# Moving A's norms and transposes, B's first operands and C's heads in the order in which a two-layer encoder trunk is emitted

## The chip, the cores and the metric

The kernel runs on one core of one Trainium2 chip. The metric is the device time of one execution in microseconds (us), as a median of several runs. TensorE (PE in the rows; PEld is its weight load) multiplies matrices into PSUM, VectorE (DVE) and ScalarE (ACT) read PSUM and work elementwise, GpSimd (POOL) works elementwise on SBUF alone, and SyncE's queue (SPq) starts the DMAs.

## The reference

A trunk of two layers over x of 512 rows and 1024 columns, in float32. Each layer normalises x, projects it once and feeds three attention branches with the parts of the projection. Their outputs are gated, merged and projected, a squared-ReLU MLP follows, and a final norm ends the trunk.

```python
for l in range(DEPTH):                      # DEPTH = 2
    h = _rms_norm(x, ln1_g[l])
    proj = jnp.einsum('bsd,dn->bsn', h, w_in[l])
    (a_q, a_k, a_v, b_q, b_k, b_v, c_cq, c_ckv, c_kr, gate_logits) = _split_columns(proj)
    y_a = _gqa_axial(...)        # 8 q heads, 2 kv heads, width 64: RMS norm of q and k per head, rotary, softmax
    y_b = _diff_attention(...)   # 8 heads, two softmaxes of width 32 each, p0 - lam * p1
    y_c = _mla(...)              # q and k, v from normalised ranks 384 and 256; a rotary part of 32 beside 64
    gates = jax.nn.sigmoid(gate_logits.reshape(b, s, N_BRANCH, d))
    merged = jnp.sum(gates * jnp.einsum('bsne,ned->bsnd', y, w_branch[l]), axis=2)
    x = x + jnp.einsum('bsd,de->bse', merged, w_out[l])
    h2 = _rms_norm(x, ln2_g[l])
    ff = jnp.square(jax.nn.relu(jnp.einsum('bsd,df->bsf', h2, w_ff1[l])))
    x = x + jnp.einsum('bsf,fd->bsd', ff, w_ff2[l])
return _rms_norm(x, final_g)
```

## The kernel before

**Numbers.** Every float32 operand of a matmul is split into a high part (a cast to the matmul's float32r, `hi`, on ScalarE) and a low part (operand less high part, `lo`, on VectorE). A product is three matmuls: high by high, high by low, low by high. A weight is fetched by SyncE into `wr` (2 buffers), cast by ScalarE into `wh` (L61) and subtracted into `wl` (L67), by VectorE in one piece of 1024 columns or by GpSimd in four of 256; `POOLW` of every five weights go to GpSimd.

**The plan.** `plan` (L996) makes a list of items, each with a cost in us of TensorE's time, a function that emits its instructions, and its weights. `run` (L153) goes through the list with a clock `t` that adds the costs. Ahead of each item it emits weight fetches up to 8 us and splits up to 3 us ahead, then all functions whose due time has come (`tick`), then the item. `defer(dt, f)` enters f with due time t + dt. `want(d, k)` (L146) runs the entered functions in the order of their due times until key k is there. `weave` mixes a list of attention items with a list of matmul items in proportion to their costs. All this sets the order of emission. The tile framework takes the emitted instructions, finds what depends on what, and lays down the order of each engine.

**Stages of a layer.** First A's k, v and C's rotary key in one projection (`a_kv`, L520, eight items of 1.458 us), then q of A's two groups (`a_q`, L482, two times eight items of 1.296), then q and k of B's first half (`b_qk`). A's scores (`att_a`, 32 items of 1.3) are woven with the rest of B's projections, B's scores (`att_b`) with the first gates and C's ranks, rotated q (`c_rope`), first values (`c_v`) and first pair, C's scores (`att_c`) with the other pairs of heads and gates. Output and MLP follow.

**A's q.** When a group's four PSUM tiles are read, `post` rotates it (`a_rope`, L453: multiplications by two tables on VectorE, half of them on GpSimd). `LAG_Q` = 14 us later `late` (L505) transposes it on TensorE (`transpose4`, L320, four matmuls each into a PSUM tile of tag T, of which there are two) and writes each pair of heads' `a_G`: two reads by ScalarE, two subtractions by VectorE (L216). At its end `late` calls `norm` (L497): the squares on GpSimd (L477), a sum on VectorE (L479), one operation (L500) and eleven small ones of `rsqrt` (L230 to L241). The result `aR[g]` is first used as the scale of the probabilities (L575, L576).

**A's k.** `post` of `a_kv` norms and rotates k and leaves `a_kr` (L549); `LAG_KV` = 14 us later `late` (L552) transposes it and splits it into `a_K` (L211 on ScalarE, L218 on VectorE).

**B.** `b_stack(h)` (L704) puts together the operands of head h, twelve DMAs from SBUF to SBUF for `b_sq` and `b_sk`. The first item of `att_b` emits `b_stack(0)` and `b_stack(1)`, the first item of each later head the next one.

**C.** `c_rope` projects the rotary part of q, rotates it (`c_t`, L880), and 6 us later transposes and splits it into two tiles `c_qr`. `c_pair(j)` (L901) projects two heads of q (`uq`) and of k (`uk`), each into a PSUM tile of tag L, of which there are three; the gates, branches and value chunks use the same three. For each head it reads the head's half of the tile two times on ScalarE, subtracts once on VectorE and copies the rotary part in by DMA.

Of the kernel before, what the change touches and what calls it, by code (L numbers as in the profile page):

```python
# [127 lines left out]
class Trunk:  # L128
# [353 lines left out]
    def a_q(self, l, g):  # L482

        nc = self.nc
        st = {}

        def evac(tt, ps):
            if tt == 0:
                st["t"] = self.s4("a_tq", (128, 4, 256), F32)
            nc.scalar.copy(st["t"][:, tt], ps)  # L490

        def post():
            t1, t2 = self.a_rope(st["t"], 4, "q")
            nc.vector.tensor_tensor(t1, t1, t2, op=ALU.add)
            st["r"], st["f"] = t1, t2

        def norm():  # L497
            ss = self.head_sumsq(nc.gpsimd, st["t"], st["f"], 4)
            v = ss.rearrange("p (t h) -> p t h", h=4)
            nc.vector.scalar_tensor_tensor(  # L500
                v, v, 1.0 / 64, self.evar.unsqueeze(2).to_broadcast([128, 4, 4]), op0=ALU.mult, op1=ALU.add)
            self.aR[g] = self.p.tile([128, 16], F32, tag="a_R", name="a_R", bufs=2)
            self.rsqrt(self.aR[g], ss, 16)

        def late():  # L505
            for j in range(2):
                T = self.transpose4(st["r"], slice(j * 128, (j + 1) * 128))
                G = self.s4("a_G")
                self.hi(G[0:64, 0], T[0:64])
                self.hi(G[64:128, 1], T[64:128])  # L510
                self.lo(G[64:128, 0], T[0:64], G[0:64, 0])
                self.lo(G[0:64, 1], T[64:128], G[64:128, 1])
                self.aG[2 * g + j] = G
            norm()

        k = P_TM[f"q{g}"]
        return self.tm_chunk([self.big(l, k), self.big(l, k + 1)], 4, 256, "x", evac, post, late, self.LAG_Q,
                             self.TAGQ if g == 0 else "LL")

# [115 lines left out]
    def att_a(self):  # L635
        self.y = {}

        def probs(h, qt):
            g, j, e = h // 4, h // 2, h % 2
            q = slice(qt * 128, (qt + 1) * 128)  # L640
            G, K = self.want(self.aG, j), self.want(self.aK, g)
            i = qt * 4 + h % 4
            p, z = self.probs([(G[:, e, q], K[:, 0]), (G[:, e, q], K[:, 1])], self.aR[g][:, i : i + 1])
            self.normalise(p, z)
            return p

        def vt(h):
            o = 64 * (h % 2)
            return lambda k: self.aV[h // 4][:, k, o : o + 128]

        return self.attend(probs, vt, self.finish_plain("a"), 1.3)
# [63 lines left out]
    def att_b(self, l):  # L715
        nc = self.nc

        def probs(h, qt):

            if h == 0 and qt == 0:  # L720
                self.b_stack(0)
            if qt == 0 and h < 7:
                self.b_stack(h + 1)
            q = slice(qt * 128, (qt + 1) * 128)
# [138 lines left out]
    def c_rope(self, l):  # L863
# [22 lines left out]
                self.split(f, T)  # L886
                self.qr[j] = f

        return self.tm_chunk([Weight(self, self.a["w768"][3 * l + 2], 768)], 3, 256, "q", evac, post, late, 6.0)

    def c_v(self, l, hb):
        def evac(tt, ps):
# [8 lines left out]
    def c_pair(self, l, j):  # L901
# [5 lines left out]
        def q():  # L907
            ps = self.ps("L", "uq")
            self.mm(ps, self.fm_pairs(w, 0, self.want(self.cf, "q")))
            for e in range(2):  # L910
                Q = self.s4("c_Q")
                r, o = (slice(0, 64), slice(64, 128)) if e == 0 else (slice(64, 128), slice(0, 64))
                self.hi(Q[r, 0], ps[r])
                self.hi(Q[r, 1], ps[r])
                self.lo(Q[o, 0], ps[r], Q[r, 0])
                h = 2 * j + e
                rr = (h % 4) * 32
                for part in range(2):
                    self.copy(Q[o.start + 32 * part : o.start + 32 * part + 32, 1], self.want(self.qr, h // 4)[rr : rr + 32, part])
                self.cQ[h] = Q  # L920

        def k():
            ps = self.ps("L", "uk")
            self.mm(ps, self.fm_pairs(wk, 0, self.want(self.cf, "kv")))
            for e in range(2):
                K = self.s4("c_K")
                r, o = (slice(0, 64), slice(64, 128)) if e == 0 else (slice(64, 128), slice(0, 64))
                self.hi(K[r, 0], ps[r])
                self.hi(K[o, 0], ps[r])
                self.lo(K[r, 1], ps[r], K[r, 0])  # L930
                self.copy(K[o, 1], self.kr[o, 0])
                self.cK[2 * j + e] = K

        return [(9 * 0.216, q, [w]), (6 * 0.216, k, [wk])]

    def att_c(self):
        def probs(h, qt):
            q = slice(qt * 128, (qt + 1) * 128)
            Q, K = self.cQ[h], self.cK[h]
            p, z = self.probs([(Q[:, 0, q], K[:, 0]), (Q[:, 1, q], K[:, 1]), (Q[:, 1, q], self.krl[:, h % 2])],  # L940
                              self.rq[:, qt : qt + 1])
            self.normalise(p, z)
# [53 lines left out]
    def plan(self, l):  # L996
# [29 lines left out]
        fb1 = self.b_qk(l, "q", 1) + self.b_qk(l, "k", 1) + self.b_v(l, 1)  # L1026
        r += fb[: self.FB]
        r += [(0, lambda: setattr(self, "POOLW", self.PA), [])]
        r += weave(self.att_a(), fb[self.FB :] + fb1)
        gb = [[self.gate_branch(l, n, d) for d in range(8)] for n in range(3)]  # L1030
        att = self.att_b(l)
        gates = lambda n, d0, d1: sum(gb[n][d0:d1], [])
# [176 lines left out]
    def go(self):  # L1209
# [5 lines left out]

        self.AHEAD_F, self.AHEAD_S = 8.0, 3.0
        self.LAG_T, self.LAG_V, self.LAG_C = 5.5, 6.0, 9.0
        self.LAG_Q, self.LAG_KV, self.LAG_R = 14.0, 14.0, 60.0

        self.P0, self.PA, self.PF = 1, 5, 0  # L1220
        self.FB = 16
# [134 lines left out]
```

## Time and profile before

| | us |
|---|---|
| median of 3 runs | 1881.75 (1879.80 to 1882.43) |
| profiled execution | 1881.45 |
| its span, first to last instruction | 1879.70 |
| TensorE busy | 1821.7 |
| VectorE busy | 1422.4 |
| ScalarE busy | 1009.8 |
| GpSimd busy | 398.3 |

The profile is one execution on the chip. A view of waits names an engine's instruction, what ended the idle time in front of it, the total, the number of times and the longest. A timeline gives start and duration of merged instructions in us, the line of the kernel, the operation, the tile written and the tiles read, the shape and the count; idle time in front stands in brackets with its releaser. A releaser is inferred from semaphores: where it names the reader of a PSUM tile, the instruction waited for that tile to come free.

### The profile page before, as it was taken

The page shows a single profiled execution, that of the slowest core. Times are in us where ns is not written, and L with a number is a line of the kernel's source. Part 1 is how long each engine was busy: PE and PEld are TensorE (multiplying, and loading weights), DVE is VectorE, ACT ScalarE, POOL GpSimd, SP SyncE. Part 2 cuts the span into 40 slices and gives each one's busy share as a digit, 9 for nine tenths or more (in the row PEclk, how much of TensorE's full clock was granted, in tenths as well). Part 3 has the DMA queues.
Part 4 walks back from the last instruction along what each step waited for, and adds up shares of the span by engine and source line. Part 5 has one row for each costly group of instructions (what it writes and reads, how often), then busy time and mean ns, then how long its engine had stood idle before and what let it go on. Part 6 is the DMA issues. An engine that isn't in the chain of part 4 may idle for free.

```text
span 1879.7 us, 29631 instructions
## 1 busy us (share of the span) xinstructions
PE 1821.7 (97%) x10960; PEld 1600.8 (85%) x10960; DVE 1422.4 (76%) x2815; ACT 1009.8 (54%) x1828; POOL 398.3 (21%) x493
## 2 busy tenths in 40 slices
PE   8999999999999999999999999999999999999997
PEld 8998787777888898989899988778878888989897
DVE  7888889755665776868888888896556767778687
ACT  5577666655544434444445766665554444443553
POOL 4322433444101000000043224434440000000000
PEclk9999999999999999999999999999999999999999
DMA  5213341332153232242332134312232522423321
GB/s 163 79 40 85 102 107 43 96 88 86 40 180 90 74 118 82 88 139 74 98 106 69 46 94 120 90 48 85 84 90 67 164 90 68 135 62 120 114 77 62
DMA packets 67776, 172.06 MB, mean 92 GB/s; under 512 B 10032, under 2 KB 14512, under 8 KB 67632
## 3 DMA queue, kind: packets, MB, share of 16 engines
q1 hardware_dynamic: 67632, 170.16, 30.3%
q8 instruction: 87, 1.43, 0.3%
q14 instruction: 57, 0.47, 0.1%
HBM read 149.15 MB, written 4.19 MB: 82 GB/s over the span
## 4 chain that ended last, share of the span: by engine, by line
PE 72%; DVE 15%; ACT 5%; DMA 4%; issue 3%; POOL 1%; SPq 0%; DVEq 0%; ACTq 0%; POOLq 0%
PE ff L208 19%; PE gate L208 12%; PE ff L1136 11%; PE br L208 6%; PE tm L295 4%; PE out L208 4%; PE sc L208 4%; PE pv L208 4%; PE pT L587 3%; DMA wr<-w 2%; PE c_rank L208 2%; DVE fl L99 2%; DVE fa L93 1%; DVE wl L67 1%; DVE mx L571 1%
## 5 line engine op out<-in xcount | busy, mean ns | idle before, releaser
L67 POOL TENSOR_TENSOR wl<-wr,wh 128x256 fp32r<-128x256 f32 (+1 forms) x402 | 297.7, 770 | 541.2 <-ACT wh L61 523.8
L61 ACT CAST wh<-wr 128x1024 fp32r<-128x1024 f32 (+5 forms) x246 | 224.6, 914 | 344.4 <-PE ff L208 94.0
L1136 PE MATMUL ff<-h,fh 128*128 128x256 f32 x1792 | 327.7, 285 | 3.7 <-ACT fh L98 3.5
L208 PE MATMUL ff<-xg,wh 128*128 128x512 f32 x1024 | 316.1, 390 | 1.8 <-ACT wh L61 1.8
L1136 PEld LDWEIGHTS ff<-h,fh 128*128 128x128 f32 x1792 | 281.0, 192 | 6.9 <-ACT fh L98 5.7
L1136 PE MATMUL ff<-h,fl 128*128 128x256 f32 x896 | 255.2, 286 | 3.0 <-DVE fl L99 3.0
L208 PE MATMUL gate<-xg,wh 128*128 128x512 f32 x768 | 242.6, 394 | 1.1 <-DVE c_K L216 1.1
L98 ACT CAST fh<-fa 128x640 fp32r<-128x640 f32 (+1 forms) x168 | 125.4, 762 | 206.8 <-PE ff L1136 122.1
L208 PEld LDWEIGHTS ff<-xg,wh 128*128 128x128 f32 x1024 | 191.6, 188 | 41.9 <-ACT wh L61 2.6
L338 POOL TENSOR_TENSOR acc<-acc,sq 128x512 f32<-128x512 f32 x15 | 25.4, 1695 | 834.8 <-ACT sq L336 832.3
L208 PE MATMUL ff<-xg,wl 128*128 128x512 f32 x512 | 199.7, 390 | 2.1 <-DVE wl L67 2.1
L295 PE MATMUL tm<-wh,xg 128*128 128x256 f32 x1024 | 201.6, 288 | 0.0
L571 DVE TENSOR_REDUCE mx<-sc 128x1 f32<-128x512 f32 x256 | 173.8, 683 | 36.3 <-PE sc L208 35.3
L1136 PEld LDWEIGHTS ff<-h,fl 128*128 128x128 f32 x896 | 172.1, 192 | 5.2 <-DVE fl L99 4.5
L208 PEld LDWEIGHTS gate<-xg,wh 128*128 128x128 f32 x768 | 143.6, 189 | 30.2 <-PE pv L208 1.4
L67 DVE TENSOR_TENSOR wl<-wr,wh 128x1024 fp32r<-128x1024 f32 (+3 forms) x117 | 134.1, 1146 | 42.6 <-ACT wh L61 42.3
L295 PEld LDWEIGHTS tm<-wh,xg 128*128 128x128 f32 x1024 | 163.9, 191 | 0.2
L99 DVE TENSOR_TENSOR fl<-fa,fh 128x640 fp32r<-128x640 f32 (+1 forms) x168 | 143.3, 864 | 10.3 <-ACT fh L98 10.3
L208 PE MATMUL gate<-xg,wl 128*128 128x512 f32 x384 | 150.9, 393 | 0.0
L590 ACT CAST pt<-pT 128x512 fp32r<-128x512 f32 x192 | 111.8, 585 | 64.3 <-PE pT L587 62.3
L591 DVE TENSOR_TENSOR pt<-pT,pt 128x512 fp32r<-128x512 f32 x192 | 131.3, 686 | 19.6 <-ACT pt L590 17.9
L295 PE MATMUL tm<-wl,xg 128*128 128x256 f32 x512 | 144.7, 283 | 0.0
(246 smaller groups left out, 3530.2 us busy)
## 6 DMA issues: line engine op xcount, KB each, us to landing
wr<-w SPq DMA_DIRECT2D x170, 512.0 KB, 3.6
fa<-wff SPq DMA_DIRECT2D x64, 320.0 KB, 3.1
wr<-w SPq DMA_DIRECT2D x52, 256.0 KB, 2.8
fa<-wff SPq DMA_DIRECT2D x32, 384.0 KB, 3.3
b_sq<-b_f SPq DMA_DIRECT2D x96, 64.0 KB, 3.0
b_sk<-b_f SPq DMA_DIRECT2D x96, 64.0 KB, 2.0
x<-xT SPq DMA_DIRECT2D x8, 256.0 KB, 5.5
c_Q<-c_qr SPq DMA_DIRECT2D x32, 64.0 KB, 2.9
```

The lines of the kernel that those rows point to most:

```text
L61: t.nc.scalar.copy(wh, self.raw)
L67: e.tensor_tensor(wl[:, q], self.raw[:, q], wh[:, q].bitcast(F32), op=ALU.subtract)
L98: t.nc.scalar.copy(h, x)
L99: t.nc.vector.tensor_tensor(lo, x, h.bitcast(F32), op=ALU.subtract)
L208: self.nc.tensor.matmul(out, l, r, start=(i == 0), stop=(i == n - 1))
L295: self.nc.tensor.matmul(ps, l, r, start=(u == 0 and i == 0 and tt % 2 == 0), stop=(u == 1 and tt % 2 == 1 and i == len(p) - 1))
L338: e.tensor_tensor(st[d % 2], st[d % 2], sq, op=ALU.add)
L571: nc.vector.tensor_reduce(m, s, axis=AX.X, op=ALU.max, negate=True)
L587: nc.tensor.transpose(T[:, k], p[:, k * 128 : (k + 1) * 128], self.ident)
L590: nc.scalar.copy(h[:, :, q], T)
L591: nc.vector.tensor_tensor(lo[:, :, q], T, h[:, :, q].bitcast(F32), op=ALU.subtract)
L1136: nc.tensor.matmul(bk[tag], x, y, start=(new and a == 0), stop=(part[1] == n and a == len(pairs) - 1), skip_group_check=True)
```

## The change

- `LAG_KV` goes from 14.0 to 16.5, the lag of `c_rope` from 6.0 to 8.0.
- `norm` of A's q is no longer called at the end of `late` but entered with a due time 6 us later. `att_a` asks for `aR` by `want`.
- `b_stack(0)` is emitted as an item of its own, three items ahead of the end of the woven list of A's scores, instead of in the first item of B's scores.
- In `c_pair` both rotary tiles of q are asked for ahead of the heads. The first head of q and of k is emitted at once, the second 2.5 us later. `att_c` asks for `cQ` and `cK` by `want`.

```diff
@@ a_q, late @@
                 self.aG[2 * g + j] = G
-            norm()
+            self.defer(6.0, norm)
@@ att_a, probs @@
-            p, z = self.probs([(G[:, e, q], K[:, 0]), (G[:, e, q], K[:, 1])], self.aR[g][:, i : i + 1])
+            R = self.want(self.aR, g)
+            p, z = self.probs([(G[:, e, q], K[:, 0]), (G[:, e, q], K[:, 1])], R[:, i : i + 1])
@@ att_b, probs @@
-            if h == 0 and qt == 0:
-                self.b_stack(0)
@@ c_rope @@
-        return self.tm_chunk([Weight(self, self.a["w768"][3 * l + 2], 768)], 3, 256, "q", evac, post, late, 6.0)
+        return self.tm_chunk([Weight(self, self.a["w768"][3 * l + 2], 768)], 3, 256, "q", evac, post, late, 8.0)
@@ c_pair, q @@
-            for e in range(2):
+            want = [self.want(self.qr, (2 * j + e) // 4) for e in range(2)]
+
+            def head(e):
                 Q = self.s4("c_Q")
...
-                    self.copy(Q[o.start + 32 * part : o.start + 32 * part + 32, 1], self.want(self.qr, h // 4)[rr : rr + 32, part])
+                    self.copy(Q[o.start + 32 * part : o.start + 32 * part + 32, 1], want[e][rr : rr + 32, part])
                 self.cQ[h] = Q
+
+            head(0)
+            self.defer(2.5, lambda: head(1))
@@ c_pair, k @@
-            for e in range(2):
+            def head(e):
...
+            head(0)
+            self.defer(2.5, lambda: head(1))
@@ att_c, probs @@
-            Q, K = self.cQ[h], self.cK[h]
+            Q, K = self.want(self.cQ, h), self.want(self.cK, h)
@@ plan @@
-        r += weave(self.att_a(), fb[self.FB :] + fb1)
+        a = weave(self.att_a(), fb[self.FB :] + fb1)
+        r += a[:-3] + [(0, lambda: self.b_stack(0), [])] + a[-3:]
@@ go @@
-        self.LAG_Q, self.LAG_KV, self.LAG_R = 14.0, 14.0, 60.0
+        self.LAG_Q, self.LAG_KV, self.LAG_R = 14.0, 16.5, 60.0
```

## Rows read from the trace of the kernel before

**Rows 1.** The page's engine table: busy us, share of the span, instructions.

```profile
PE 1821.7 (97%) x10960; PEld 1600.8 (85%) x10960; DVE 1422.4 (76%) x2815; ACT 1009.8 (54%) x1828; POOL 398.3 (21%) x493
```

**Rows 2.** TensorE's waits, whole span: us in total, times, longest.

```profile
PE tp L324 <- DVE a_G L216: 4.0, 2, 2.1
...
PE tp L324 <- DVE a_kr L549: 2.6, 2, 1.5
...
PE gate L208 <- DVE c_K L216: 1.1, 2, 0.6
...
PE pT L587 <- DVE c_qr L216: 0.7, 2, 0.4
...
PE tm L208 <- DVE c_K L216: 0.4, 2, 0.2
```

**Rows 3.** Busy us in a stretch: length, PE, PEld, DVE, ACT, POOL, clock, DMA.

```profile
46.00:71.00 25.00, 22.88 (x193) 22.56 (x192) 23.05 (x49) 11.47 (x20) 8.00 (x10) 1.00 0.29 85
```

**Rows 4.** VectorE's waits from 25 to 75 us, all of them.

```profile
DVE b_f L218 <- ACT b_f L211: 1.1, 1, 1.1
DVE ss L479 <- POOL a_t L477: 0.8, 1, 0.8
DVE a_V L218 <- ACT a_V L211: 0.2, 1, 0.2
```

**Rows 5.** VectorE's timeline, A's preparation: start, duration, line, operation.

```profile
45.22 1.28 DVE L218 SCALAR_TENSOR_TENSOR a_K<-tp,a_K 128x512 fp32r<-128x512 f32 x2
47.31 1.22 DVE L479 TENSOR_REDUCE ss<-a_t 128x16 f32<-128x1024 f32 x1 [0.81 <-POOL a_t L477]
...
52.56 0.67 DVE L236 SCALAR_TENSOR_TENSOR rsy<-rst,rsy 128x16 f32<-128x16 f32 x1
53.26 0.17 DVE L237 TENSOR_TENSOR rst<-rsy 128x16 f32<-128x16 f32 x1
...
54.19 1.22 DVE L459 TENSOR_TENSOR a_t<-a_tq,tabs 128x1024 f32<-128x1024 f32 x1
...
67.32 2.81 DVE L216 TENSOR_TENSOR a_G<-tp,a_G 64x512 fp32r<-64x512 f32 x4
...
77.05 0.69 DVE L571 TENSOR_REDUCE mx<-sc 128x1 f32<-128x512 f32 x1 [4.41 <-PE sc L208]
```

**Rows 6.** TensorE's timeline, A's preparation: the transposes that wait.

```profile
40.16 1.09 PE L324 MATMUL tp<-ident,a_kr 128*128 128x128 f32 x8 [1.13 <-DVE a_kr L549]
...
68.86 0.63 PE L324 MATMUL tp<-ident,b_t 128*128 128x128 f32 x4 [2.12 <-DVE a_G L216]
```

**Rows 7.** GpSimd's timeline, A's preparation.

```profile
45.38 1.90 POOL L477 TENSOR_TENSOR a_t<-a_tq 128x1024 f32<-128x1024 f32 x1 [2.16 <-DVE a_t L494]
...
50.37 2.82 POOL L67 TENSOR_TENSOR wl<-wr,wh 128x256 fp32r<-128x256 f32 x4
```

**Rows 8.** SyncE's queue ahead of B's scores: start, time in the queue, DMAs.

```profile
148.45 10.07 SPq L53 DMA_DIRECT2D wr<-w  x2
158.57 3.78 SPq L221 DMA_DIRECT2D b_sq<-b_f  x6
```

**Rows 9.** TensorE's timeline at B's first score.

```profile
171.53 0.40 PE L208 MATMUL sc<-b_sk,b_sq 96*128 96x512 f32 x1
```

**Rows 10.** ScalarE's timeline at C's first pair.

```profile
334.27 1.07 ACT L211 ACTIVATE c_Q<-uq 64x512 fp32r<-64x512 f32 x2
335.23 1.06 ACT L211 ACTIVATE c_qr<-tp 128x512 fp32r<-128x512 f32 x2
...
340.42 1.20 ACT L211 ACTIVATE c_K<-uk 64x512 fp32r<-64x512 f32 x2
```

**Rows 11.** TensorE's timeline at C's first pair: what waits.

```profile
337.38 0.63 PE L587 MATMUL pT<-ident,p 128*128 128x128 f32 x4 [0.36 <-DVE c_qr L216]
...
342.50 0.47 PE L208 MATMUL gate<-xg,wh 128*128 128x512 f32 x1 [0.56 <-DVE c_K L216]
```

**Rows 12.** VectorE's timeline at C's first pair.

```profile
341.66 0.69 DVE L216 TENSOR_TENSOR c_K<-uk,c_K 64x512 fp32r<-64x512 f32 x1 [1.48 <-ACT c_K L211]
```

## The prediction

> **What bounds the kernel now.** I read the page's engine table first: TensorE is busy 1821.7 of 1879.7 us [rows 1]. No edit here takes a matmul away, so only TensorE's idle time can shrink, 58.0 us by that row. Next, the list of TensorE's waits over the whole run, which says who ends that idle time [rows 2]. The places that the edits reach have a row each: the transposes of A's rotated k (2.6 us, two times, one in each layer), the transposes of b_t that wait until VectorE has read the PSUM of a_G (4.0, two), a probability transpose that waits for c_qr (0.7, two), a gate and a value projection that wait for c_K (1.1 and 0.4, two each). Together 8.8 us, 0.47% of the run. Both layers show the same waits at the same places, so I work layer 0 out and double it.
>
> Then the stage itself. From 46 to 71 us VectorE is busy 23.05 of 25 us, TensorE 22.88 [rows 3]; and in the whole stretch 25 to 75 VectorE waited three times, 1.1, 0.8 and 0.2 us, and the 1.1 lies after a_G's reads [rows 4]. So **VectorE, not TensorE, sets the end of A's preparation**: it works from one row to the next, and TensorE's 1.13 us in front of the k transposes and its 2.12 us in front of b_t [rows 6] are two parts of one slack.
>
> One more reading decides much. The instructions of an engine don't stand in the order in which the program emits them. The squares of q0's norm run on GpSimd at 45.38 [rows 7] and its sum on VectorE at 47.31, while the rotation of q1, emitted earlier, follows at 54.19 [rows 5]. The norm is emitted only behind q0's transposes, yet it runs when its data are there. Emission therefore acts as a preference among what is ready, and an edit to it moves an instruction only where something else was ready too.
>
> **The change, part by part.** The base is the profiled execution, 1881.45 us: span 1879.70 and 1.75 around it. The median of the runs is 1881.75, 0.30 above; I add the sum to the median.
>
> *A's k, LAG_KV 14 to 16.5.* In the planner's time the eight rows of kv take 8 x 1.458 = 11.66, each q item 1.296. Due at 25.66 the transposes ran ahead of the item that starts at 25.92; due at 28.16 they run ahead of the one at 28.51, two items (24 matmuls, 2.6 in the planner's us) later. a_kr is there at 40.16, TensorE stood ready at 39.03, so behind two items the 1.13 us wait is gone [rows 6]. But TensorE then only reaches the b_t transposes 1.13 us sooner, and a_G's four subtractions still begin at 67.32, because VectorE has no idle time to give [rows 4, 5]. I take 0. Below: all of the 2.6 us. Above: the two subtractions of a_K at 45.22 (1.28 us) fill part of a gap that ends when GpSimd has squared q0 [rows 5, 7]; if they come ready too late and stand behind the sum at 47.31, the whole VectorE chain is 1.28 us later, 2.6 for both layers. The row nearest to the value is that of VectorE's waits, hence 0.
>
> A page's rule bears on that upper bound. A norm operation of 128x16 takes 0.67 us at 52.56 and 0.17 at 53.26 [rows 5], and GpSimd's weight subtraction lies at 50.37 to 53.19 [rows 7]. The Trainium skill, page "SBUF — State Buffer", section "Who interferes with whom", says that a VectorE instruction with two SBUF inputs contends with a GpSimd one that reads SBUF, and one with at most one SBUF input doesn't. The trace agrees: the norm operation has two, and a subtraction out of PSUM at 341.66 takes 0.69 us in a stretch in which GpSimd subtracts weights [rows 12]. By that rule a_K's subtractions, put behind the sum, would push about two norm operations of layer 0 out of GpSimd's stretch, 2 x 0.50 = 1.0 us back, and the upper bound would be 1.6 instead of 2.6.
>
> *The norms of A's q, deferred by 6.* Norm 0 goes from 34.99 to 41.47 in the planner's time, norm 1 from 45.36 to 51.84: past the reads of two PSUM chunks by ScalarE, one weight split, and for norm 1 the transposes of bq0 and the fetch of a bv0 weight (on SyncE's queue; the norm itself issues no DMA). If norm 1 really left VectorE's order ahead of a_G's reads, the 4.0 us wait [rows 2] would be gone. But nothing that it is moved past is a_G's read: those are emitted ahead of the norm already, and the norm runs first because its data are there first. I take 0; below 4.0, above 0, as norm 0 has until head 0's first scale and norm 1 until head 4, and before the first scores VectorE stands idle for 4.41 us [rows 5].
>
> *B's first operands, three items earlier.* Twelve DMAs on SyncE's queue. They stand directly behind the fetch of the first gate's weight at 148.45 to 158.52, the first six from 158.57 in 3.78 us, so twelve in about 7.6 [rows 8]. Between old and new place no other DMA is emitted, so the queue's order stays. TensorE shows no idle time where the first score of B stands, at 171.53 [rows 9]. 0; if they did pass the fetch they would use up to 7.6 us in which the queue waits.
>
> *C's rotated q, lag 6 to 8.* The first pair asks for it before either lag has run out (it starts 4.87 of the planner's us after the projection's last item began: that item 0.97, four value chunks of 0.65, a score of 1.3), so it runs at the same call. 0.
>
> *C's heads one by one.* In the pair the wanted c_qr now comes ahead of the first head, and the second head of Q and of K 2.5 later: two reads by ScalarE, one subtraction and two copies (K: one copy) each, behind the next item. The copies fall behind a weight fetch on SyncE; the second head's scores come a whole head later, which hides them. On ScalarE at 334.27 the reads of c_Q (1.07) go first, then c_qr (1.06), and c_K's second pair of reads is at 340.42 [rows 10]; with c_qr's first read (half of 1.06) done while uq is still multiplying, everything behind it is 0.53 us earlier. TensorE's 0.36 us for c_qr and 0.56 us for c_K [rows 11] are nearly of that size. I take both: 0.7 + 1.1 = 1.8 us over two layers. Above, if a bank is held longer: see the slower rival.
>
> Sum: 0 + 0 + 0 + 0 - 1.8, so 1881.75 - 1.8 = **1879.9**.
>
> **Rivals.** *A pays too.* Both waits of A go, because the norm of q1 does leave VectorE's way: -2.6 - 4.0 - 1.8 = -8.4, 1873.3. For it: the two sit within one chain, and the norm of q1, a sum of 1.22 us like that at 47.31 and twelve small operations, lies ahead of a_G's reads. Against: readiness, shown above. *Nothing moves.* The engines' orders are as before: 1881.75. For it: the same reading, applied to the heads. *The held bank, slower.* uq, uk, gates and value chunks share three PSUM banks. The gate at 342.50 and a value chunk in the third pair already wait for c_K (0.56 and 0.20 at most, [rows 2, 11]), so there each delay of the second head of K is a delay of TensorE. If that head loses its place on ScalarE to one other pair of reads (1.20, [rows 10]), it costs 1.2 x 2 places x 2 layers = 4.8, and the gain isn't had: 1886.6. It decides as soon as the second head's reads stand behind any other head's. Against it: reads of the same bank become ready together, with little else ready at 336 to 340.
>
> **How the numbers follow.** This kernel's measurement can tell about 0.2%, 3.8 us, from no change: 1878.0 to 1885.5. The forecast has 0.50 (1877 to 1884 with the bounds of k), A pays too 0.25, nothing moves 0.12, the held bank 0.13. Faster: 0.25 and 0.05 of the forecast's lower edge, 0.30. Slower: 0.10 of the held bank. Same: 0.60. The range reaches to the two outer cases, 1873.3 to 1886.5, and leaves out about half of each, some 2 in 10. The forecast's own range is 1877 to 1884.
>
> **What would show it.** In the profile after: the k transposes two items further back with no wait (right in any case); the wait of b_t for a_G some 3.2 us instead of 2.1 in layer 0 (my zero for k), or gone (A pays too); the norm's sum still directly behind a_G of q0 on VectorE; c_qr ahead of c_Q on ScalarE, and the c_qr and c_K rows gone from TensorE's waits; a longer wait of gate or value chunk for c_K is the held bank. If the wait for a_G shrinks, my reading of readiness is wrong.

## The result and the profile after

The changed kernel takes **1886.47 us** (median; 1882.21 to 1888.98), the kernel before beside it 1881.51: a ratio of 1.0028, with a 95% interval of 1.0016 to 1.0039, so 3 to 7 us slower. Run once more beside other kernels it was 1.0036 (1.0024 to 1.0048). The forecast was 1879.9, 1.8 us faster. The profiled execution took 1886.47, its span 1884.7.

The span is 5.0 us longer. TensorE's busy time grew by 1.1 us of these ([rows 1] has 1821.7); in the other 3.9 it stood:

```profile
PE 1822.8 (97%) x10960; PEld 1600.6 (85%) x10960; DVE 1419.0 (75%) x2815; ACT 1009.8 (54%) x1828; POOL 399.6 (21%) x493
```

TensorE's waits over the whole run of the changed kernel (engine, line, what ended the wait: us in total, times, longest):

```profile
PE tp L324 <- DVE a_G L216: 6.4, 2, 3.3
...
PE sc L208 <- ACT p L576: 4.6, 4, 1.2
...
PE bss L208 <- ACT bsq L741: 1.8, 2, 0.9
...
PE tm L208 <- DVE c_Q L216: 0.8, 2, 0.4
PE tp L324 <- DVE a_K L218: 0.7, 1, 0.7
```

The rows of [rows 2] for a_kr, for the gate on c_K and for the probability transpose on c_qr are gone. In their place the wait for a_G has grown from 4.0 to 6.4, and there are waits for bsq, c_Q and a_K. (bsq holds the squares of B's outputs, which bss sums for B's last norm; bR and bT, met further down, carry that norm back to the outputs.) The places on TensorE's timeline of the changed kernel (start, length, instruction, idle time ahead and what ended it):

```profile
41.91 1.04 PE L324 MATMUL tp<-ident,a_kr 128*128 128x128 f32 x8
...
69.09 1.09 PE L324 MATMUL tp<-ident,b_t 128*128 128x128 f32 x4 [3.11 <-DVE a_G L216]
...
350.57 0.64 PE L208 MATMUL pv<-pt,b_V 128*128 128x256 f32 x4
...
355.94 1.05 PE L208 MATMUL bss<-blk,bsq 128*128 128x2 f32 x8 [0.87 <-ACT bsq L741]
...
399.94 0.35 PE L208 MATMUL tm<-wh,c_f 128*128 128x256 f32 x1 [0.39 <-DVE c_Q L216]
...
402.00 0.73 PE L208 MATMUL sc<-c_K,c_Q 128*128 128x512 f32 x2 [1.13 <-ACT p L576]
...
979.75 1.04 PE L324 MATMUL tp<-ident,a_t 128*128 128x128 f32 x6 [0.71 <-DVE a_K L218]
...
998.87 0.63 PE L324 MATMUL tp<-ident,b_t 128*128 128x128 f32 x4 [3.32 <-DVE a_G L216]
```

**A's stage.** The k transposes no longer wait (41.91; 40.16 with 1.13 us in [rows 6]). The 1.13 us have moved into the wait for a_G, 3.11 instead of 2.12. In layer 1 a wait of 0.71 comes on top: q0's transposes wait for a PSUM bank that a_K still holds. And the four transposes behind the 3.11 us took 1.09 us, where they took 0.63 before. The windows there show why (stretch, length, TensorE busy, granted clock, DMA share, GB/s), first the changed kernel:

```profile
69.00:70.00 1.00, 0.91 (x5) 0.50 0.65 262
70.00:71.00 1.00, 1.00 (x6) 0.50 0.49 197
```

and one window of the kernel before:

```profile
70.00:71.00 1.00, 1.00 (x10) 1.00 0.23 94
```

A granted clock of 0.50 is the level of 1.2 GHz: six matmuls from 70 to 71 instead of ten. In layer 1 such a stretch follows the 3.32 us too, from 1000.3 on.

**C's first two pairs.** TensorE's stretch from the first uq to the third pair's first uq took 58.24 and 58.21 us in the two layers before (331.77 to 390.01 and 1261.60 to 1319.81), and takes 59.21 and 59.25 now (333.17 to 392.38 and 1263.36 to 1322.61). ScalarE of the changed kernel in it:

```profile
333.32 0.59 ACT L211 ACTIVATE c_qr<-tp 128x512 fp32r<-128x512 f32 x1
...
336.48 0.60 ACT L211 ACTIVATE c_qr<-tp 128x512 fp32r<-128x512 f32 x1 [0.35 <-PE tp L324]
...
340.86 1.20 ACT L211 ACTIVATE c_K<-uk 64x512 fp32r<-64x512 f32 x2
342.08 1.07 ACT L211 ACTIVATE c_Q<-uq 64x512 fp32r<-64x512 f32 x2
343.06 1.04 ACT L61 CAST wh<-wr 128x1024 fp32r<-128x1024 f32 x1
...
350.82 1.05 ACT L61 CAST wh<-wr 128x1024 fp32r<-128x1024 f32 x1 [2.34 <-DMA wr<-w]
351.90 1.08 ACT L211 ACTIVATE c_Q<-uq 64x512 fp32r<-64x512 f32 x2
...
353.65 0.58 ACT L600 COPY fx<-pv 64x512 f32<-64x512 f32 x1
...
355.25 0.63 ACT L741 ACTIVATE bsq<-yt 128x512 f32<-128x512 f32 x1
```

and of the kernel before:

```profile
339.35 1.05 ACT L61 CAST wh<-wr 128x1024 fp32r<-128x1024 f32 x1
340.42 1.20 ACT L211 ACTIVATE c_K<-uk 64x512 fp32r<-64x512 f32 x2
...
349.16 1.05 ACT L61 CAST wh<-wr 128x1024 fp32r<-128x1024 f32 x1
350.23 0.58 ACT L600 COPY fx<-pv 64x512 f32<-64x512 f32 x1
...
351.84 0.63 ACT L742 ACTIVATE bsq<-yt 128x512 f32<-128x512 f32 x1
```

In the kernel before ScalarE's queue was full: it was busy 16.90 of the first 17.66 us of this stretch. Two windows of the stretch follow, up to the probability transposes at 349.43 and from there to the gate behind bss (stretch, length, then the busy time of TensorE, its weight loads, VectorE, ScalarE and GpSimd, granted clock, DMA share, GB/s), first of the kernel before:

```profile
331.77:349.43 17.66, 16.74 (x81) 13.28 (x81) 13.74 (x29) 16.90 (x35) 6.13 (x9) 1.00 0.58 149
349.43:354.69 5.26, 5.09 (x29) 4.07 (x28) 4.51 (x10) 4.37 (x8) 4.21 (x6) 1.00 0.13 19
```

and the same two of the changed kernel:

```profile
333.17:351.04 17.87, 17.58 (x81) 13.07 (x81) 13.68 (x28) 14.51 (x31) 6.29 (x9) 1.00 0.42 119
351.04:356.85 5.81, 4.94 (x29) 3.98 (x28) 3.31 (x6) 5.69 (x10) 4.25 (x6) 1.00 0.38 94
```

The two waits that are gone lay in the first window. TensorE's idle time there fell from 0.92 to 0.29 us, but its busy time for as many matmuls grew from 16.74 to 17.58, so the window is 0.21 us longer and not 0.92 shorter. One place of the growth can be named: behind the gate's first matmuls, at 344.95, TensorE's weight load waits 0.51 us for GpSimd's `wl`. The second window, with bss, is 0.55 us longer, and the rest of the stretch 0.21.

The split of a weight (wh, L61) stood directly behind pt at 339.35; now it stands at 343.06, behind a pair of reads each of c_K and c_Q: 3.7 us later, of which 1.4 are those by which the changed kernel is late here, from A's stage. GpSimd finishes that weight later, and its buffer is needed by the next weight fetch, so this one is issued by SyncE later. GpSimd's timeline of the changed kernel, at that weight:

```profile
344.17 2.99 POOL L67 TENSOR_TENSOR wl<-wr,wh 128x256 fp32r<-128x256 f32 x4 [7.08 <-ACT wh L61]
```

SyncE's queue of the changed kernel, the fetch behind it (two, the first at 347.19):

```profile
347.19 3.16 SPq L53 DMA_DIRECT2D wr<-w  x2
```

and SyncE's queue of the kernel before, the same fetch:

```profile
343.31 0.33 SPq L53 DMA_DIRECT2D wr<-w  x1
```

GpSimd ends at 347.16 and the fetch follows at 347.19; before, it was issued at 343.31. That is 3.9 us later, 2.5 without the 1.4. ScalarE then stands 2.34 us in front of the split of that weight at 350.82, and behind it stand the second head of c_Q, the gate, fx and bsq. At the end of this chain TensorE waits 0.87 us for bsq (0.17 before). Without the 1.4 us the split at 350.82 starts only 0.25 us later than the one at 349.16, but bsq 2.0: the second head of c_Q (1.08) and a weight split that stood behind bsq now stand ahead of it. This chain is read off the trace; no run here undid one link of it alone. B's last value matmuls, of which bsq is made, now run behind gate matmuls at 350.57; before, they were done ahead of the gate at 342.50 [rows 11].

### The profile page after: what moved, and what is told of

It reads as the page before. It is cut to its first block, busy times and chain, and to the rows that moved or that the text cites. A ratio compares the mean times of both kernels' runs of the same rounds, so it can differ in the third digit from the quotient of the medians.

```text
span 1884.7 us, 29635 instructions
## 1 busy us (share of the span) xinstructions
PE 1822.8 (97%) x10960; PEld 1600.6 (85%) x10960; DVE 1419.0 (75%) x2815; ACT 1009.8 (54%) x1828; POOL 399.6 (21%) x493
## 4 chain that ended last, share of the span: by engine, by line
PE 73%; DVE 16%; ACT 4%; DMA 3%; issue 3%; POOL 1%; SPq 0%; DVEq 0%; ACTq 0%; POOLq 0%
PE ff L208 18%; PE gate L208 12%; PE ff L1144 12%; PE br L208 6%; PE tm L295 5%; PE out L208 4%; PE sc L208 4%; PE pT L587 4%; PE pv L208 3%; DMA wr<-w 3%; PE c_rank L208 2%; DVE fl L99 2%; DVE fa L93 1%; ACT wh L61 1%; DVE wl L67 1%
## 5 line engine op out<-in xcount | busy, mean ns | idle before, releaser
L61 ACT CAST wh<-wr 128x1024 fp32r<-128x1024 f32 (+5 forms) x246 | 224.9, 914 | 355.9 <-PE ff L208 94.7
```

The source lines that it names most:

```text
L61: t.nc.scalar.copy(wh, self.raw)
```

## The experiments

The edits are made to the kernel before, e12's to the changed kernel (e11 is the changed kernel itself); each run is compared with the kernel before on the same chip. The last column is the mean, over a kernel's runs, of the granted clock of a run.

| run | edit | median us | ratio (95%) | mean clock (runs) |
|---|---|---|---|---|
| e1 | LAG_KV 16.5 | 1882.23 | 1.0011 (1.0001, 1.0020) | 0.9943 (11) |
| e2 | C's edits | 1888.36 | 1.0039 (1.0027, 1.0052) | 0.9916 (5) |
| e3 | c_qr first | 1883.18 | 1.0012 (1.0002, 1.0022) | 0.9953 (11) |
| e4 | the three other edits | 1881.09 | 0.9995 (0.9982, 1.0008) | 0.9944 (11) |
| e5 | second heads later | 1887.47 | 1.0045 (1.0030, 1.0061) | 0.9932 (6) |
| e6 | norm behind by its data | 1877.41 | 0.9979 (0.9968, 0.9990) | 0.9960 (12) |
| e7 | e6 and LAG_KV 16.5 | 1875.08 | 0.9972 (0.9960, 0.9985) | 0.9962 (6) |
| e8 | e1, matmuls in A's wait | 1886.53 | 1.0040 (1.0027, 1.0052) | 0.9938 (5) |
| e9 | c_qr first, Q's second head later | 1884.65 | 1.0013 (1.0002, 1.0024) | 0.9942 (12) |
| e10 | c_qr first, K's second head later | 1884.79 | 1.0015 (1.0005, 1.0025) | 0.9945 (11) |
| e11 | the change again | 1888.55 | 1.0036 (1.0024, 1.0048) | 0.9924 (9) |
| e12 | the change and e6 | 1880.85 | 0.9995 (0.9984, 1.0006) | 0.9934 (11) |
| e13 | C's edits, first two pairs | 1884.18 | 1.0011 (1.0001, 1.0020) | 0.9947 (12) |
| e14 | C's edits, last two pairs | 1881.73 | 1.0001 (0.9992, 1.0009) | 0.9944 (12) |
| e15 | matmuls in C's wait | 1884.32 | 1.0011 (1.0002, 1.0021) | 0.9949 (12) |
| e16 | e7 and e15 | 1876.68 | 0.9973 (0.9962, 0.9984) | 0.9967 (7) |

**e1, A's k alone.**

```
-        self.LAG_Q, self.LAG_KV, self.LAG_R = 14.0, 14.0, 60.0
+        self.LAG_Q, self.LAG_KV, self.LAG_R = 14.0, 16.5, 60.0
```

> The kernel before with LAG_KV 16.5 alone (A's k transposes two items later), all else as before. Theory 1, two idle stretches become one that is long enough to bring the granted clock down: TensorE's idle of 1.13 us ahead of the k transposes goes, the one ahead of b_t grows from 2.12 to 3.1 us (layer 0) and from 1.86 to 3.3 (layer 1), and behind each of them stands a stretch of 1.2 GHz that the kernel before doesn't have there. +0.2 us for the later VectorE chain and 1.1 to 1.5 us for the slow matmuls, a layer: 2.6 to 3.4 us slower than before, 1884.1 to 1884.9 beside 1881.5. Theory 2, the edit of k is worth nothing (the step of the prediction) and the whole loss is C's: 0 us, 1881.5. Theory 3, only the VectorE chain: 0.2 us a layer, 0.5 us.

Slower by 0.2 to 3.8 us, median 0.8. Both waits for a_G are there (3.12 and 3.31 us), but only layer 1 shows the 1.2 GHz behind it. Theory 1 was too sure of the clock: e1's mean clock is that of the kernel before beside it (0.9943). Theory 2's 0 lies just outside the interval, theory 3's 0.5 us inside.

**e2, C's edits alone.**

```
-            for e in range(2):
+            want = [self.want(self.qr, (2 * j + e) // 4) for e in range(2)]
+            def head(e):
...
+            head(0)
+            self.defer(2.5, lambda: head(1))
```

> The kernel before with the edits of C's pairs alone (c_qr asked for first, second head of Q and of K 2.5 later), all else as before. Theory 1 (both A and C lose): 2.0 us slower in each layer up to the end of the third pair, part of it given back behind, so 2 to 3 us slower than before, 1883.5 to 1884.5 beside 1881.5. Theory 2 (the loss is C's alone): 5 us slower, 1886.5. The prediction's step: 1.8 us faster, 1879.7.

5 to 10 us slower, at the upper of the two sizes; the prediction's step has the wrong sign. The mean clock is the lowest of all, and the profiled execution has nine stretches of 1.2 GHz ahead of its end, where the kernel before has three; it is the slowest of the five runs.

**e3, c_qr asked for first.**

```
+            want = [self.want(self.qr, (2 * j + e) // 4) for e in range(2)]
             for e in range(2):
                 Q = self.s4("c_Q")
...
-                    self.copy(Q[...], self.want(self.qr, h // 4)[rr : rr + 32, part])
+                    self.copy(Q[...], want[e][rr : rr + 32, part])
```

> The kernel before with one thing of C's edits alone: the wanted c_qr is asked for ahead of the first head of Q; both heads of Q and of K still leave PSUM together. If the prediction's gain was right and only the later second heads cost: 1.0 to 1.8 us faster than before, TensorE's waits for c_qr (0.36 us) and c_K (0.56) in the first pair gone, 1879.7 to 1880.5 beside 1881.5. If asking for c_qr first is itself what moves the first pair's order the wrong way: 1 us slower or more, with the wait of bss for bsq (0.17 before, 0.87 after) at its new length.

Slower by 0.4 to 4.1 us. The waits for c_qr and c_K are gone as the prediction had it, and a new one is there, 1.13 us of bT for bR; the two pairs' stretch is 59.74 us in layer 1 instead of 58.21 (60.01 in layer 0, with a stretch of 1.2 GHz in it). So the very step that was to bring the gain costs.

**e4, the three other edits.**

```
-            norm()
+            self.defer(6.0, norm)
...
+        r += a[:-3] + [(0, lambda: self.b_stack(0), [])] + a[-3:]
...
-  ... "q", evac, post, late, 6.0)
+  ... "q", evac, post, late, 8.0)
```

> The kernel before with the three other edits (norms of A's q deferred by 6, B's first operands three items earlier, lag of C's rotated q 8). Both theories and the prediction: no engine's work moves, so 0 us, 1881.5, within 0.1 per cent. The norm's sum stands directly behind a_G of q0 on VectorE as before, and TensorE's wait for a_G stays 2.1 and 1.9 us. Another result would show that the norm's place does count.

No change, as all had it: every engine has the same instructions in the same order as before.

**e5, the second heads later, without c_qr first.**

```
-            for e in range(2):
+            def head(e):
...
+            head(0)
+            self.defer(2.5, lambda: head(1))
```

> The kernel before with the other half of C's edits alone: the second head of Q and of K 2.5 later, c_qr asked for where it was before (at the copies of each head). The stretch of TensorE from the first uq of a layer to the uq of its third pair took 58.24 us in the kernel before, 59.74 with c_qr asked for first, 59.2 with both. If the two halves simply add: 57.7 to 58.2 in that stretch, at most 0.6 more behind it, so within 1 us of before, 1881 to 1882.5 beside 1881.5. If the later second heads cost by themselves (a value chunk of the third pair waits for a bank that the second head of Q still holds, 0.39 us, and a score 1.13 instead of 0.70): 1 to 1.5 us a layer, 1883.5 to 1884.5.

5.6 to 11.5 us slower: not additive. The stretch is 59.67 and 59.74 us, and bss waits 1.64 us for bsq in layer 0. The chain is that of the changed kernel: the fetch comes at 346.93, and ScalarE stands 1.83 us in front of the split at 350.57.

**e6, the norm held back by its data.**

```
-            ss = self.head_sumsq(nc.gpsimd, st["t"], st["f"], 4)
+            ss = self.head_sumsq(nc.gpsimd, st["t"], st["r"], 4)
```

> The kernel before, where the squares of A's q norm are written over the rotated q (st r) and not over the spent half of the rotation (st f). The transposes read the rotated q, so the sum can't run before they have: the norm is moved by its data and not by its place in the emission. If the prediction's reading is right (the norm ran ahead because its data were there first, and it stands in a_G's way): a_G of q0 about 5 us earlier on VectorE, TensorE's wait for a_G (2.12 and 1.86 us) gone in both layers, 4.0 us, and with it up to 1.6 us for the slow stretches that stood behind it in about half of the layers seen: 1876 to 1877.5 beside 1881.5. Rival, another wait takes its place (the first scales of A wait for a_R, or b_f's bank): less than 1 us, 1880.5 to 1881.5.

3.9 us faster by the ratio (1.9 to 6.0). VectorE's timeline of e6:

```profile
49.42 1.23 DVE L459 TENSOR_TENSOR a_t<-a_tq,tabs 128x1024 f32<-128x1024 f32 x1 [1.30 <-ACT a_tq L490]
...
54.78 2.81 DVE L216 TENSOR_TENSOR a_G<-tp,a_G 64x512 fp32r<-64x512 f32 x4
57.63 1.22 DVE L479 TENSOR_REDUCE ss<-a_t 128x16 f32<-128x1024 f32 x1
...
65.68 0.68 DVE L216 TENSOR_TENSOR a_G<-tp,a_G 64x512 fp32r<-64x512 f32 x1 [1.19 <-ACT a_G L211]
```

and TensorE's wait for a_G in it, from 30 to 82 us:

```profile
PE tp L324 <- DVE a_G L216: 0.2, 1, 0.2
```

The rotation of q1 begins at 49.42 (54.19 in [rows 5]), the first sum stands behind a_G, and a_G's reads for q1 begin at 65.68 (67.32), now held up by ScalarE. The wait for a_G is 0.2 us instead of 2.1 in layer 0, and 1.0 instead of 1.9 in layer 1.

**e7, e6 with LAG_KV 16.5** (the lines of e6 and of e1).

> As the run before it, and LAG_KV 16.5 with it (A's k transposes two items later). If VectorE is no longer what A's preparation ends on: both waits of A go, 2.6 and 4.0 us, 6.6 together, 1873.5 to 1875 beside 1881.5 (the prediction's case in which A pays too, without its 1.8 of C). Rival, TensorE comes 1.13 us sooner to a_G and waits there again: as the run before it, 1876 to 1877.5.

5.7 us faster in the median (2.8 to 7.5), the lowest median here. The k wait is gone too and does not come back at a_G (0.2 and 1.0 us), so by the waits the edit of k pays once VectorE no longer sets the end. The times alone don't show it: the intervals of e6 and e7 overlap.

**e8, matmuls that nobody reads in A's wait.**

```
             t = st["t"]
+            if n == "q" and hb == 0:
+                w = self.ps("V", "keep")
+                for _ in range(13):
+                    self.mm(w, [(self.xg[0][:, 0, 0:128], self.xg[0][:, 0])])
```

> LAG_KV 16.5 alone, and 13 matmuls whose sum nobody reads (128x512, 0.23 us each, 3.0 us) on TensorE directly ahead of the b_t transposes, where it otherwise waits 3.1 to 3.3 us for a_G. They add work that the reference doesn't have and change no output. Theory 1 (the slow stretch behind that wait comes from the idle time): no stretch of 1.2 GHz at 69 and 1000 us in any layer, A's stretch as short as the shortest seen with this LAG_KV (70.25 us in layer 0), 0.8 to 1.7 us faster than LAG_KV 16.5 alone, 1880.5 to 1881.5 beside 1882.2. Theory 2 (the slow stretches come whatever TensorE does): 1882 or more, and one of them stands behind the added matmuls as often as before.

Slower than e1, by 4.3 us in the medians and 5.5 by the ratios, and no clean test of the clock. The matmuls filled 65.32 to 68.45, but both groups of four transposes now followed one another and each still waited. TensorE's timeline of e8:

```profile
65.32 3.13 PE L208 MATMUL keep<-xg 128*128 128x512 f32 x13
69.32 0.63 PE L324 MATMUL tp<-ident,b_t 128*128 128x128 f32 x4 [0.86 <-DVE a_G L216]
70.74 0.63 PE L324 MATMUL tp<-ident,b_t 128*128 128x128 f32 x4 [0.79 <-DVE a_G L216]
```

Behind these two waits no stretch of 1.2 GHz followed. In layer 1 one followed from 1004.1 on, behind waits of 1.07 and 0.80 us, so theory 1 did not come true as it was put.

**e9 and e10, one of the two second heads later.** e2 with this in k (e9) or in q (e10):

```
-            self.defer(2.5, lambda: head(1))
+            head(1)
```

> The kernel before with c_qr asked for first and the second head of Q alone 2.5 later; both heads of K leave PSUM together as before. Theory Q (the bank of uq, held by the second head of Q, is what the later places wait for): the value chunk of the third pair waits 0.39 us for c_Q, the score behind it 1.1, and bss for bsq 0.8 or more; C costs 1.2 to 1.7 us a layer as with both, 1884 to 1885 beside 1881. Theory K (the prediction's rival, the second head of K): those waits are as in the kernel before, 0.70 and below, and C costs what c_qr first costs, at most 1.5 us a layer.

> The kernel before with c_qr asked for first and the second head of K alone 2.5 later; both heads of Q together as before. Theory Q: the third pair's value chunk doesn't wait for c_Q, its score waits 0.7 as before. Theory K (the prediction's rival): a gate of the first pair or a value chunk of the third waits 1 us or more for c_K, and the kernel is about 5 us slower than before, 1886.

0.4 to 4.7 us slower, and both theories fall: with Q's head alone later the third pair's value chunk waits for c_K, and a uk of the first pairs 1.0 us for c_K; with K's alone bT waits for bR as in e3. TensorE's waits from 332 to 407 us of e9:

```profile
PE tm L208 <- DVE c_K L216: 1.4, 1, 1.4
```

and from 331 to 407 of e10:

```profile
PE bT L762 <- DVE bR L755: 1.2, 1, 1.2
```

It is not one head's bank; each order of ScalarE's reads tried here has a late reader somewhere.

**e11, the change again; e12, the change with e6's line** (`st["r"]` for `st["f"]` in norm).

> The changed kernel itself once more, beside the two runs before it. All theories: 0.16 to 0.39 per cent slower than before, 1884 to 1888.5 beside 1881. If its waits in C are of its program and not of one execution: bss for bsq 0.87 us, the third pair's value chunk for c_Q 0.39, the score 1.13 in both layers again. The stretches of 1.2 GHz may stand elsewhere: they were in other places in every execution looked at.

> The changed kernel with A's squares written over the rotated q as in the run of that name, so with A's waits gone. If the loss of the changed kernel is A's k (0.8 to 2 us) and C's heads (2.5 to 3.5 us), each in its own place, then this kernel differs from the one with the norm behind and LAG_KV 16.5 (1875.1) by C's part alone: 1877.5 to 1879. If C's part is 5 us or more by itself, as the run with C's edits alone had it: 1880 to 1882.

e11's time is as expected; bss waits 0.73 and 0.67 us, the value chunk 0.38 and 0.40. The stretches of 1.2 GHz did not stand elsewhere: three of e11's four ahead of its end, at 68.6, 1000.4 and 1392.9 us, are those of the first profile of the changed kernel, and one at 911.7 has come. e12 against e7 is C's part alone: 0.9995 and 0.9972 of the kernel before, 0.0023 or 4.3 us, but with both intervals 1 to 7 us, which leaves both sizes open. e12's mean clock is 0.0028 below e7's.

**e13 and e14, C's edits by pairs.** e2 with this in q and k (e13; in e14 `j > 1`, and there the first two pairs ask for c_qr where they did before):

```
-            self.defer(2.5, lambda: head(1))
+            self.defer(2.5, lambda: head(1)) if j < 2 else head(1)
```

> The kernel before with C's edits in the first two pairs of each layer alone: c_qr asked for first, second heads 2.5 later; in the third and fourth pair both heads together. If the loss is in the first two pairs (ScalarE's order there: a weight split behind the heads' reads, the next weight's fetch 2.4 us later, bss behind it): the stretch from the first uq to the third pair's 59.2 us or more instead of 58.2, bss waits 0.9 us for bsq, the third pair's waits as in the kernel before (0.70 at most), 2 us slower or more, 1883.5 to 1886 beside 1881.5. If it is in the later pairs: within 1 us of before.

> The kernel before with C's edits in the third and fourth pair alone, the first two as before. If the loss is in the first two pairs: 58.2 us in their stretch, and 0.3 to 1 us a layer from the third pair's waits (value chunk for c_Q 0.39, score 1.13, value chunk for c_V 0.46, together 2.0, where the kernel before has 1.4), 1881.5 to 1883. If it is in the later pairs: 1884 or more.

TensorE's waits from 331 to 407 us, of e13:

```profile
PE bss L208 <- ACT bsq L742: 0.9, 1, 0.9
```

and of e14, from 330:

```profile
PE sc L208 <- ACT p L576: 1.1, 1, 1.1
...
PE tm L208 <- DVE c_V L216: 0.5, 1, 0.5
PE tm L208 <- DVE c_Q L216: 0.4, 1, 0.4
```

The loss is in the first two pairs: e13's stretch there is 59.34 us in layer 1 (58.21 before; 59.57 in layer 0, with a stretch of 1.2 GHz in it) and the kernel is 2.1 us slower by the ratio (0.2 to 3.8), the size of those 1.1 us twice. The last two pairs show their three waits, 2.0 us together, and cost nothing: the kernel before has waits of 1.4 us at the same place, and from the third pair's first uq to the fourth's e14 takes 54.79 and 54.78 us, the kernel before 54.73 and 54.77.

**e15 and e16, matmuls that nobody reads in C's longest wait.**

```
         T = self.ps("T", "pT", (128, 4, 128))
+        for _ in range(fill):
+            self.mm(T.rearrange("p a b -> p (a b)"), [(self.xg[0][:, 0, 0:128], self.xg[0][:, 0])])
```

(fill is 10 for C's head 4, third block of rows, and 0 elsewhere; e16 has the edits of e6 and e1 with it.)

> The kernel before, with 10 matmuls (128x512, 0.23 us each) on TensorE ahead of the probability transposes that wait 2.6 and 2.3 us for p in C (head 4, third block of rows); they write the PSUM bank that the transposes then overwrite, add work that the reference doesn't have, and change no output. If the slow stretches behind that wait come from TensorE's idle time: none there in either layer, a mean granted clock about 0.0007 to 0.001 above that of the kernel before (0.9945), 1 to 2.5 us faster, 1879 to 1880.5 beside 1881.5. If they come whatever TensorE does: the clock as before, 1881.5 to 1882.

> The three things that ought to shorten the kernel before, together: A's norm behind its transposes, LAG_KV 16.5, and the 10 matmuls in C's wait. Added up 5.7 us for the first two (measured) and 0 to 2.5 for the third: 1873 to 1876 beside 1881.5, with no slow stretch in A or behind C's wait in either layer.

No stretch of 1.2 GHz stands behind that wait in the four layers, but e15 is slower, 0.4 to 4 us. The bank comes free late, and the added matmuls then run beyond the end of the old wait: the transposes behind them start at 462.78, where those of the kernel before start at 459.63, or 461.6 with the 2.0 us by which e15 is late at C. TensorE's timeline of e15:

```profile
460.42 2.52 PE L208 MATMUL pT<-xg 128*128 128x512 f32 x10 [1.48 <-DVE pt L593]
```

Four layers prove nothing by themselves, as the wait without them is followed by the slow clock only about half of the time (18 of 32 layers of the other executions). e16 is as fast as e7 within the intervals.

## Why the prediction was wrong, step by step

**The step that failed is "C's heads one by one", the term of -1.8 us.** Its order came true: c_qr's reads (333.32 and 336.48, both and not only the first) run ahead of c_Q's (336.97), and both waits are gone. But they gave no time back: where they stood, TensorE's busy time grew by 0.84 us. What the step left out is a third kind of instruction in ScalarE's queue. The prediction counted the reads of c_Q, c_qr and c_K and moved them against each other; the weight splits stand in the same queue, their buffers decide when SyncE can issue the next fetch, and the next split holds up everything behind it. ScalarE was busy 16.90 of 17.66 us from 331.77 on in the kernel before, a row that the prediction did not read, so it was an engine with no room, as VectorE is in A. 58.2 us became 59.2 a layer, +2.0 instead of -1.8; 0.55 of the 1.0 us lies at the new wait, bss for bsq, and 0.21 on either side of it. e13 shows the loss in the first two pairs, and e14 finds none in the others. Either half loses by itself: e5 by the same chain, e3 by another (no wait for a fetch at the split; bT waits 1.13 us for bR).

**The rival of the held bank** had the sign and, at 1886.6, the size, but not the way: the gate of the first pair no longer waits for c_K, the value chunk of the third waits 0.39 us for c_Q and not for c_K, and e14 shows that this costs nothing. The argument against it had looked at the reads of one bank and not at the splits that stand among them. In e9, with Q's second head alone later, a bank that c_K holds does cost.

**A's k, taken at 0.** The wait of 3.2 us was forecast and is 3.11. The bound that was set aside came true: a_K's subtractions stand behind the norm's sum. VectorE's timeline of the changed kernel:

```profile
45.31 1.22 DVE L67 TENSOR_TENSOR wl<-wr,wh 128x1024 fp32r<-128x1024 f32 x1
48.31 1.22 DVE L479 TENSOR_REDUCE ss<-a_t 128x16 f32<-128x1024 f32 x1 [1.79 <-POOL a_t L477]
49.45 1.28 DVE L218 SCALAR_TENSOR_TENSOR a_K<-tp,a_K 128x512 fp32r<-128x512 f32 x2
...
53.30 0.17 DVE L236 SCALAR_TENSOR_TENSOR rsy<-rst,rsy 128x16 f32<-128x16 f32 x1
...
67.55 0.68 DVE L216 TENSOR_TENSOR a_G<-tp,a_G 64x512 fp32r<-64x512 f32 x1
```

and GpSimd's, the squares of q0:

```profile
45.47 2.81 POOL L477 TENSOR_TENSOR a_t<-a_tq 128x1024 f32<-128x1024 f32 x1 [2.16 <-DVE a_t L494]
```

Yet a_G begins only 0.23 us later (67.55, 67.32 in [rows 5]) and not 1.28. VectorE's weight subtraction moved ahead to 45.31, and the norm's operations fell out of GpSimd's weight stretch: 0.17 us at 53.30, where the one at 52.56 took 0.67. But the weight subtraction now runs beside GpSimd's squares, which take 2.81 us instead of 1.90 [rows 7], so the sum starts 1.0 later. The Trainium skill, page "SBUF — State Buffer", section "Who interferes with whom", names just this pair, a VectorE instruction with two SBUF inputs beside a GpSimd one that reads SBUF, and the trace agrees on both sides of the account: the prediction used the rule for what leaves the stretch and not for what enters it. Its other half, that an operation with at most one SBUF input doesn't contend, does not hold as the prediction shortened it: in the kernel before such an operation (L232) took 0.67 us at 50.47, in GpSimd's weight stretch, and 0.17 at 980.54, where GpSimd subtracts no weight. The page limits that half to operations outside VectorE's 2-port modes. The other miss is "I work layer 0 out and double it": in layer 1 a_K held its bank for 0.71 us. Together the waits of A's stage are 7.1 us instead of 6.6. The clock behind a longer wait was not thought of; whether it costs is not shown, as e1's mean clock did not fall. Measured, k costs 0.2 to 3.8 us.

**Right:** the norm's defer, B's first operands and the lag of C's rotated q at 0 (e4, same orders); the reading that emission is only a preference among ready instructions; and, through e6, that the norm of q1 stands ahead of a_G and that this wait is time lost: e6 is 3.9 us faster once the norm's data hold it back. That this is so near to the 4.0 is partly luck, as the wait for a_G shrank by 2.7 us and was not gone. "A pays too" is what e7 did; the change did not, because a deferred emission does not move an instruction that is ready.

**What stays open.** By the ratios the changed kernel is 5.3 and 6.8 us slower (the first result and e11), k alone 2.1 (e1; 0.8 by the medians), C's first two pairs 2.1 and its last two 0.2 (e13, e14). But C's edits in all four pairs are 4.3 (e12 against e7) to 7.3 (e2). What is left goes in part with the granted clock: 0.9941 and 0.9924 in the two sets of runs of the changed kernel, 0.9945 in 109 runs of the kernel before. By those runs (below) 0.001 is some 1.3 us, so 0.5 us in the first set and 2.7 in e11. Why the clock is lower with all four pairs edited, and not with two (0.9947 and 0.9944), no run here tells. And the two profiles that are compared here show as many stretches of 1.2 GHz, three ahead of their ends: of the 5.0 us between them 2.0 are C's first two pairs, and 2.2 lie behind the fourth pair's first uq of layer 1, a part that took 505.1 us before, 507.3 in the changed kernel and 503.1 to 508.0 in the other executions. No run explains those 2.2.

## What to carry to other kernels

Before moving one engine's reads against each other, list everything that stands in that engine's queue in the stretch, the weight splits too, and follow what each one frees: here a buffer that came free 2.5 us later delayed a fetch, and the fetch held up the queue that was to be relieved. In this kernel deferring an emission moved only what was not ready (e4 left every engine's order as it was); to move a ready instruction out of the way, give it a real dependence, as by writing over a buffer that the urgent work still reads. Two waits on one chain are one slack: removing the first made the second longer here, and the stage's waits came to 7.1 us instead of 6.6. A wait that is gone from the list is not yet time gained: look at the busy time and the length of the same stretch too.

## What the runs showed of the hardware that was not expected

The times of one and the same kernel follow its granted clock. The 109 runs of the kernel before that stood beside these experiments:

| granted clock of the run | 0.992 | 0.993 | 0.994 | 0.995 | 0.996 | 0.997 |
|---|---|---|---|---|---|---|
| runs | 3 | 18 | 36 | 27 | 23 | 2 |
| mean us | 1887.4 | 1883.7 | 1882.6 | 1880.9 | 1879.7 | 1877.8 |

That is some 1.3 us for 0.001 of the clock from 0.993 to 0.996. Most of the stretches of 1.2 GHz come back at a few places, near 69, 332, 461, 912, 1000 and 1390 us; which of them an execution shows differs. Behind TensorE's wait for a_G a stretch of 1.2 GHz followed in 10 of 20 layers where the wait was 1.8 to 2.1 us, in 5 of 6 where it was 3.1 to 3.3, and in none of 8 where it was at most 1.1 (e6, e7, e12, e16). e8, whose transposes waited two times in each layer, is not in these counts; one of its two layers had such a stretch. So at this place a wait of 1.8 us or more went, half of the time or more often, with slow matmuls behind it. That the wait is their cause is not shown: e8 and e15 were to test it and don't decide it. e6's 3.9 us (1.9 to 6.0) for a wait that shrank by 2.7 us fits such a cost and does not prove it; the wait for a_kr of layer 1, which was 0.47 to 1.55 us in the executions that have it, was also 1.0 us shorter in e6's than in that of the kernel before.
